# A fourth pair of split-weight buffers in place of the attention's features by token, and moved pick-ups, in a one-core hybrid decoder layer

## The chip, the core and the metric

One core of one Trainium2 chip. The metric is the device time of one launch in microseconds (us). The program uses TensorE (PE, with its weight loads shown as PEld), VectorE (DVE), ScalarE (ACT), GpSimd (POOL) and the DMA queues that SyncE (SP) and POOL feed.

## The reference

```python
def reference(x, ...):
    h = rms_norm(x, pre_norm_w)
    proj = h @ w_in                       # one projection, split in 8
    # A: gated DeltaNet: conv + SiLU on q, k, v; chunked delta rule
    #    (triangular solve per 64-chunk), gated RMSNorm
    oa = gated_delta_rule(l2(qa), l2(ka), va, beta, g)
    u_a = (rms(oa) * gdn_norm_w * silu(za)) @ w_branch_a
    # B: causal attention (one block of 256)
    ob = moba_attention(qb, kb, vb)
    u_b = (ob * silu(moba_z)) @ w_branch_b
    merged = sigmoid(gate_a) * u_a + sigmoid(gate_b) * u_b
    return x + rms_norm(merged @ w_out, post_norm_w)
```

256 tokens, model width 2048, 8 heads of 128 in each mixer, all float32.

## The kernel before

**Products.** Every large product is made of rounded halves: a number is its rounding hi plus the rest lo, and a product is hi·hi + hi·lo + lo·hi. The activations are kept in that form (hT, oaT, obT, mT). Weights are loaded in pieces of 1 MB (`raw_*`, three buffers, SP queue), and `split` (L215) makes of each half of a piece a pair: `hi_*` is a copy by ACT (L218), `lo_*` a difference by DVE (L219), both 128x1024. The pool `wspl` has three such pairs. TensorE then runs 12 matmuls of 512 columns on a pair (16 of 512 and 256 in `proj_t`), or 6 where only a quarter of the product is made. `mm` (L144) and `tr` (L147) pin TensorE's order; the copies and differences of `split` aren't pinned, and a list scheduler places them.

**Order of the work.** `ORDER` (L42) lists the blocks of the input projection. Beside them run queues (class `Queue`): `tick`, called after each half split, takes half a unit off each queue's wait and runs its next step when the wait is over. The DeltaNet's scores, its triangular inverse and its solve stand in `gq`, the attention's pairs of heads in `aq` and `bq`, the pick-ups of finished products in `dq`. The constants at the top are waits in units of two ticks.

**Triangular inverse** (`inverse`, L616). The triangles come back by DMA into `lc` on 32 partitions (`l_d`, L636). After `LC_WAIT` (L641), `copy` (L639, ACT, 1.05 us each) spreads them to the other partitions: three copies for the first 16 rows, further ones in steps 4, 7 and 10 of each 16. 63 steps of a product (L650, tw) and a difference (L657, tv) on DVE follow. The result goes to DRAM (`t_d`, L660) and back (`tt`, L666) by POOL's queue, and `solve` (L862) multiplies with it (`sv_*`, `so_*`).

**Attention** (`attend`, L1019). After `A_WAIT1` the scores `ms_*`, softmax on DVE and ACT (L1027 to L1033), after `A_WAIT2` the transposes `pp_*`, after `A_WAIT3` the values `po_*`; `turned_attention` (L1053) transposes the gated output (`pt_*`) into obT. Its features by token, `y_mq` and `y_mk`, lie in eight buffers of 1 KB (tag "f256"), which `halves` (L452) takes from the pool `wk`; L1072 multiplies the keys with rrow.

**Merged products** (`seven`, L776). Two by two blocks of a product are made from seven block products instead of eight. `branch_pair` (L825) runs it for columns 0 and 1 and again for 2 and 3 of the DeltaNet branch, with a gate projection (`ga3`, `gb2`) as fill between the seven; the output projection uses it once more. The weight differences `tq_*` are formed on DVE (L740), one of them inside `seven` by `fourth` (L792). `done` (L835) multiplies a finished product with its gate.

Of the kernel before, what the change touches and what calls it, by code (L numbers as in the profile page):

```python
# [8 lines left out]
F32 = mybir.dt.float32  # L9
F32R = mybir.dt.float32r  # L10
# [5 lines left out]
P = 128  # L16
# [8 lines left out]
D_WAIT = 7  # L25
SC_WAIT = 4
L_WAIT = 5
LC_WAIT = 2
INV = (0.6, 2)
SLOW = 8  # L30
T_WAIT = (5, 7, 7)
V_WAIT = 8
SV_WAIT = 1
OS_WAIT = 3
A_WAIT1 = 1
A_WAIT2 = 3
A_WAIT3 = 2
A_WAIT4 = 4
# [36 lines left out]
def hybrid_layer(  # L75
# [16 lines left out]
    B, S, D = x.shape  # L92
# [22 lines left out]
    wspl = ctx.enter_context(tc.tile_pool(name="wspl", bufs=3))  # L115
    wk = ctx.enter_context(tc.tile_pool(name="wk", bufs=2))
    dram = ctx.enter_context(tc.tile_pool(name="dram", bufs=1, space=bass.MemoryType.DRAM))
    acc = ctx.enter_context(tc.tile_pool(name="acc", bufs=4, space=bass.MemoryType.PSUM))
    aux = ctx.enter_context(tc.tile_pool(name="aux", bufs=4, space=bass.MemoryType.PSUM))

    def acc_tile(name):
        return acc.tile([P, 512], F32, tag="acc", name=name)
# [5 lines left out]
    aq, bq = [Queue(), Queue()], [Queue(), Queue()]  # L128
# [14 lines left out]
    def mm(*args, **kwargs):  # L143
        return pin(nc.tensor.matmul(*args, **kwargs))  # L144
# [67 lines left out]

    def split(raw, shape, name):  # L215
        hi = wspl.tile(shape, F32R, tag="hi", name=f"hi_{name}")
        lo = wspl.tile(shape, F32R, tag="lo", name=f"lo_{name}")
        nc.scalar.copy(hi, raw)  # L218
        nc.vector.tensor_tensor(lo, raw, hi.bitcast(F32), op=ALU.subtract)  # L219
        return hi, lo  # L220
# [94 lines left out]
    rrow = cst.tile([P, S], F32, name="rrow")  # L315
    prr = aux_tile("prr")
    for t in range(NT):
        dg = wk.tile([P, P], F32, tag="f256", bufs=8, name=f"dg_{t}")
        nc.vector.tensor_scalar_mul(dg, ident, rstd[:, t : t + 1])
        mm(prr[:, t * P : (t + 1) * P], ones, dg, start=True, stop=True)  # L320
    nc.vector.tensor_copy(rrow, prr[:, :S])
# [128 lines left out]


    def halves(pt, name):  # L452
        y = wk.tile([P, S], F32, tag="f256", bufs=8, name=f"y_{name}")
        nc.scalar.copy(y, pt[:, S:])
        nc.vector.tensor_tensor(y, pt[:, :S], y, op=ALU.add)
        return y
# [159 lines left out]
    def inverse():  # L616
        lc = big.tile([P, 64, 64], F32, tag="u1", name="lc")
        tv = big.tile([P, 16, 64], F32, tag="tv", name="tv")
        tw = big.tile([P, 16, 64], F32, tag="tw", name="tw")

        nc.gpsimd.memset(tv, 1.0)
        for g in range(4):
            nc.gpsimd.affine_select(
                out=tv[32 * g : 32 * g + 32],
                in_=tv[32 * g : 32 * g + 32],
                compare_op=ALU.is_equal,
                fill=0.0,
                base=g,
                pattern=[[4, 16], [-1, 64]],
                channel_multiplier=0,  # L630
            )

        rows = [slice(16 * r, 16 * r + 16) for r in range(4)]
        yield 0.5
        for js in rows:
            nc.gpsimd.dma_start(lc[0:32, js], l_d.rearrange("b h j i -> (b h) j i")[:, js])  # L636

        def copy(r, g):
            pin(nc.scalar.copy(lc[32 * g : 32 * g + 32, rows[r]], lc[0:32, rows[r]]))  # L639

        yield LC_WAIT  # L641
        for g in range(1, 4):
            copy(0, g)
        yield 0.5
        for j in range(63):
            if j < 48 and j % 16 in (4, 7, 10):
                copy(j // 16 + 1, (j % 16 - 1) // 3)
            n, r = j // 4 + 1, 63 - j
            pin(
                nc.vector.tensor_tensor(  # L650
                    tw[:, :n, :r],
                    lc[:, j : j + 1, j + 1 :].to_broadcast([P, n, r]),
                    tv[:, :n, j : j + 1].to_broadcast([P, n, r]),
                    op=ALU.mult,
                )
            )
            pin(nc.vector.tensor_tensor(tv[:, :n, j + 1 :], tv[:, :n, j + 1 :], tw[:, :n, :r], op=ALU.subtract))  # L657
            yield INV[after[0] > 0]
        for g in range(4):
            nc.gpsimd.dma_start(  # L660
                t_d.rearrange("b h (c g) i -> g (b h) c i", g=4)[g], tv[32 * g : 32 * g + 32]
            )
        inv.append(big.tile([P, NT, H, 64], F32, tag="tt", name="tt"))
        for p_ in range(2):
            for t in range(NT):
                nc.gpsimd.dma_start(  # L666
                    inv[0][p_ * 64 : p_ * 64 + 64, t, :, :], t_d[2 * t + p_].rearrange("h c i -> c h i")
                )
        yield L_WAIT
# [30 lines left out]
    def ga(c, t):  # L700
        return ga_[:, c, t, :]
# [48 lines left out]
    def product(a, raw, banks, first, name):  # L750

        for u in range(2):
            hi, lo = split(raw[:, 2 * u : 2 * u + 2, :], [P, 2, 512], f"{name}_{u}")
            for kk in range(2):
                k = 2 * u + kk
                for (ah, al), pt, new in zip(a, banks, first):
                    mm(pt, ah[:, k], hi[:, kk, :], start=(new and k == 0), stop=False, skip_group_check=True)
                    mm(pt, ah[:, k], lo[:, kk, :], start=False, stop=False, skip_group_check=True)
                    mm(pt, al[:, k], hi[:, kk, :], start=False, stop=(k == 3), skip_group_check=True)
                tick()  # L760
# [15 lines left out]
    def seven(quarter, s_, tq, w, c, banks, name, fill=lambda i: None, done=lambda b: None):  # L776
        c11, c12, c21, c22 = banks
        s5 = tq[0][:, 0]
        product([quarter(0, 0)], load(w, 0, c, name), [c21], [True], f"{name}p1")
        fill(0)  # L780
        product([s_[0]], tq[0], [c12], [True], f"{name}p5")
        nc.scalar.copy(c11, c21)
        product([s_[1]], tq[1], [c21], [False], f"{name}p6")

        dq.add(steps(lambda: nc.scalar.copy(s5, c12), lambda: nc.vector.tensor_tensor(c12, c21, s5, op=ALU.add)))
        fill(1)
        dq.drain()
        raw21 = load(w, 1, c, name)
        product([quarter(0, 1)], raw21, [c11], [False], f"{name}p2")
        product([s_[2]], tq[2], [c21], [False], f"{name}p7")  # L790

        def fourth(u):  # L792
            us = slice(2 * u, 2 * u + 2)
            pin(nc.vector.tensor_tensor(tq[1][:, us], raw21[:, us], tq[1][:, us], op=ALU.subtract))

        dq.add(
            steps(
                lambda: fourth(0),
                lambda: fourth(1),
                lambda: nc.vector.tensor_tensor(c22, c21, s5, op=ALU.add),  # L800
                lambda: done(c11),
            )
        )
        fill(2)
        product([s_[3]], load(w, 1, c + 1, name), [c12], [False], f"{name}p3")
        dq.drain()
        dq.add(steps(lambda: done(c12), lambda: done(c22)))
        fill(3)
        product([quarter(1, 1)], tq[1], [c21], [False], f"{name}p4")
        dq.add(later(lambda: done(c21)))  # L810
# [4 lines left out]

    def steps(*fs):
        for f in fs:
            f()
            yield 0.5

    def later(f):
        yield 1
        f()

    def branch_pair(i):  # L825
        c = 2 * i
        while not oas or c not in formed:
            sq.tick()
            gq.tick()
        c11, c12, c21, c22 = (acc_tile(f"a_ua{c}_{n}") for n in ("11", "12", "21", "22"))  # L830
        place = {id(c11): (c, 0), id(c12): (c + 1, 0), id(c21): (c, 1), id(c22): (c + 1, 1)}

        def done(b):
            cc, t = place[id(b)]
            nc.vector.tensor_tensor(ga(cc, t), ga(cc, t), b, op=ALU.mult)  # L835


        quarter = quarters(hT)
        n, g, col = (("ga", 3, CGA), ("gb", 2, CGB))[i]
        pts = [aux_tile(f"a_{n}{g}_{t}") for t in range(NT)]  # L840

        def gate(h):
            raw = load(w_in[:, col : col + D], h, g, n)
            product([quarter(0, h), quarter(1, h)], raw, pts, [h == 0] * 2, f"{n}{g}_{h}")
            if h == 3:
                for t in range(NT):
                    nc.scalar.activation(gate_place(n, g, t), pts[t], AF.Sigmoid, scale=rstd[:, t : t + 1])

        seven(quarters(oaT[0]), oas, tqs[-1], wa, c, (c11, c12, c21, c22), f"ua{c}", fill=gate, done=done)
# [169 lines left out]
    def attend(h, qT, kT):  # L1019
        yield A_WAIT1  # L1020
        ps = aux_tile(f"ms_{h}")
# [234 lines left out]
    for t in range(NT):  # L1256
        for k in range(KT):
            hi, lo = parts[k // 2][0][:, k % 2], parts[k // 2][1][:, k % 2]
# [35 lines left out]
```

## Time and profile before

| | before |
|---|---|
| median of 3 runs | 783.29 us (781.9 to 783.38) |
| profiled execution, its own time | 783.66 us |
| its span, first to last instruction | 781.7 us |
| mean granted TensorE clock | 0.996 |
| busy: PE, PEld, DVE, ACT, POOL | 765.8, 650.3, 564.2, 434.5, 33.5 us |
| DMA | 151.85 MB, mean 194 GB/s |

Times in rows are microseconds from the start of the span, unless a column is marked ns. A row of the timeline has start, duration, engine, line, operation, output<-inputs, shapes and count; in brackets stands the idle time of the engine before it and what ended it. A row of the waits has the engine and line, what it waited for, and then the sum, the number and the longest. A group row has count, busy time, mean ns of one, and the idle time before them with its main cause. The ends of matmuls are modelled: a 512-column matmul is shown with 0.39 us, though the next one starts 0.23 us after it, so stops are taken from start to start.

### The profile page before, as it was taken

To read this page: it belongs to the slowest core of one execution; us is meant where nothing else is said; L and a number is where in the kernel's file an instruction comes from. 1 tells how busy PE (TensorE), PEld (TensorE's weight loads), DVE (VectorE), ACT (ScalarE), POOL (GpSimd) and SP (SyncE) were. 2 spreads that over 40 slices of the span, in tenths; PEclk is the share of its full clock that TensorE was granted. 3 is DMA by queue.
4 is the path that set the end of the run, shared out by engine and by line. 5 is a ranking of instruction groups with operands and counts; after the bars stand their busy time and mean duration, and the time that the engine had idled before them with its cause. 6 is when DMAs were issued, how large, how long until landed. Compare 5 with 4: busy or idle time off the path is not lost.

```text
span 781.7 us, 10350 instructions
## 1 busy us (share of the span) xinstructions
PE 765.8 (98%) x3923; PEld 650.3 (83%) x3923; DVE 564.2 (72%) x914; ACT 434.5 (56%) x652; POOL 33.5 (4%) x61
## 2 busy tenths in 40 slices
PE   8999999999999999999999999999999999999995
PEld 7898988898788888888898888878887788887884
DVE  5787669885977898764547965675758677878753
ACT  5676665657656564553366474654455544556641
POOL 3000001112000000020001000000000000000000
PEclk9999999999999999999999999999999999999999
DMA  8576675467566556684348356657564965475822
GB/s 304 168 229 218 187 213 169 135 182 201 171 207 191 186 183 197 203 217 122 104 122 309 119 182 237 213 193 240 177 200 136 350 213 176 147 264 185 307 106 107
DMA packets 93655, 151.85 MB, mean 194 GB/s; under 512 B 3237, under 2 KB 46886, under 8 KB 93094
## 3 DMA queue, kind: packets, MB, share of 16 engines
q1 hardware_dynamic: 88902, 134.42, 53.8%
q0 software_dynamic: 4128, 15.74, 6.1%
q10 hardware_dynamic: 576, 1.05, 0.4%
q8 instruction: 30, 0.49, 0.3%
q14 instruction: 19, 0.16, 0.1%
HBM read 148.04 MB, written 3.15 MB: 193 GB/s over the span
## 4 chain that ended last, share of the span: by engine, by line
PE 89%; DVE 4%; ACT 4%; DMA 2%; issue 1%; SPq 0%; DVEq 0%; ACTq 0%
PE a_ga L144 11%; PE a_gb L144 11%; PE a_y L144 10%; PE a_k L144 6%; PE a_mk L144 6%; PE a_ub L144 6%; PE a_zm L144 6%; PE a_mq L144 5%; PE a_mv L144 5%; PE a_zg L144 5%; PE a_q L144 4%; PE a_v L144 4%; PE a_ua L144 3%; PE sv L144 2%; PE s L144 1%
## 5 line engine op out<-in xcount | busy, mean ns | idle before, releaser
L144 PE MATMUL a_ga<-hi_ga,hT 128*128 128x512 f32 x256 | 82.0, 393 | 0.0
L144 PE MATMUL a_gb<-hi_gb,hT 128*128 128x512 f32 x256 | 79.9, 389 | 0.0
L219 DVE TENSOR_TENSOR lo_gb<-raw_gb,hi_gb 128x1024 fp32r<-128x1024 f32 x32 | 38.8, 1223 | 26.6 <-ACT hi_gb L218 26.5
L144 PEld LDWEIGHTS a_gb<-hi_gb,hT 128*128 128x128 f32 x256 | 48.1, 188 | 9.9
L144 PEld LDWEIGHTS a_ga<-hi_ga,hT 128*128 128x128 f32 x256 | 48.1, 188 | 9.9
L219 DVE TENSOR_TENSOR lo_ga<-raw_ga,hi_ga 128x1024 fp32r<-128x1024 f32 x32 | 38.9, 1222 | 18.4 <-ACT hi_ga L218 18.2
L218 ACT CAST hi_gb<-raw_gb 128x1024 fp32r<-128x1024 f32 x32 | 33.3, 1052 | 33.3 <-PE a_gb L144 24.4
L144 PE MATMUL a_gb<-lo_gb,hT 128*128 128x512 f32 x128 | 50.5, 395 | 1.2 <-DVE lo_gb L219 1.1
L144 PE MATMUL a_ga<-lo_ga,hT 128*128 128x512 f32 x128 | 50.2, 392 | 1.0 <-DVE lo_ga L219 1.0
L218 ACT CAST hi_ga<-raw_ga 128x1024 fp32r<-128x1024 f32 x32 | 33.5, 1053 | 29.5 <-PE a_ga L144 15.4
L144 PE MATMUL a_zg<-hi_zg,hT 128*128 128x348 f32 (+1 forms) x192 | 47.0, 322 | 0.0
L144 PE MATMUL a_mk<-hT,hi_mk 128*128 128x512 f32 x128 | 46.5, 404 | 0.0
L144 PE MATMUL a_mq<-hT,hi_mq 128*128 128x512 f32 x128 | 46.4, 404 | 0.0
L144 PE MATMUL a_y<-hi_y,mT 128*128 128x512 f32 x144 | 45.9, 391 | 0.0
L144 PE MATMUL a_q<-hT,hi_q 128*128 128x512 f32 x128 | 45.8, 398 | 0.0
L144 PE MATMUL a_v<-hT,hi_v 128*128 128x512 f32 x128 | 45.2, 397 | 0.5 <-ACT hi_v L218 0.5
L144 PE MATMUL a_k<-hT,hi_k 128*128 128x512 f32 x128 | 41.2, 405 | 0.2 <-DVE hT L249 0.2
L144 PE MATMUL a_ub<-hi_ub,obT 128*128 128x512 f32 x128 | 41.1, 393 | 0.0
L144 PE MATMUL a_zm<-hi_zm,hT 128*128 128x512 f32 x128 | 40.6, 392 | 0.0
L144 PE MATMUL a_mv<-hi_mv,hT 128*128 128x512 f32 x128 | 40.1, 391 | 0.0
L144 PE MATMUL a_v<-hT,lo_v 128*128 128x256 f32 x128 | 36.0, 281 | 1.1 <-DVE lo_v L219 1.1
L144 PE MATMUL a_mq<-hT,lo_mq 128*128 128x256 f32 x128 | 35.9, 281 | 0.0
(377 smaller groups left out, 1973.2 us busy)
## 6 DMA issues: line engine op xcount, KB each, us to landing
raw_ga<-in_w_in_dram SPq DMA_DIRECT2D x16, 1024.0 KB, 5.2
raw_gb<-in_w_in_dram SPq DMA_DIRECT2D x16, 1024.0 KB, 6.2
raw_y<-in_w_out_dram SPq DMA_DIRECT2D x15, 1024.0 KB, 5.5
raw_q<-in_w_in_dram SPq DMA_DIRECT2D x8, 1024.0 KB, 5.8
raw_mv<-in_w_in_dram SPq DMA_DIRECT2D x8, 1024.0 KB, 5.2
raw_v<-in_w_in_dram SPq DMA_DIRECT2D x8, 1024.0 KB, 5.7
raw_zm<-in_w_in_dram SPq DMA_DIRECT2D x8, 1024.0 KB, 5.2
raw_mq<-in_w_in_dram SPq DMA_DIRECT2D x8, 1024.0 KB, 5.7
```

Source lines behind the costliest of these rows:

```text
L144: return pin(nc.tensor.matmul(*args, **kwargs))
L218: nc.scalar.copy(hi, raw)
L219: nc.vector.tensor_tensor(lo, raw, hi.bitcast(F32), op=ALU.subtract)
```

## The change

1. The 1 KB buffers (`f256`) move from `wk` to a pool `wf` of their own. At the first `branch_pair` the queues `aq` and `bq` are drained, `wf` is closed, and a pool `wx` of the same 8 KB is opened with one hi and one lo buffer. From then on every fourth `split` takes its pair from there.
2. `steps`, which runs the pick-ups one by one, waits half a unit before each of them instead of after it.
3. `LC_WAIT` goes from 2 to 3.5, and half a unit lies between the first copies instead of only behind them.
4. `A_WAIT1` goes from 1 to 1.5.
5. `fourth` inside `seven` is renamed `difference`.

The numbers of instructions are the same but for two more table loads on ACT and some semaphore waits.

```diff
-LC_WAIT = 2
+LC_WAIT = 3.5
...
-A_WAIT1 = 1
+A_WAIT1 = 1.5
...
+    early = ExitStack()
+    wf = early.enter_context(tc.tile_pool(name="wf", bufs=8))
...
+    splits, fourth = [0], []
+
     def split(raw, shape, name):
-        hi = wspl.tile(shape, F32R, tag="hi", name=f"hi_{name}")
-        lo = wspl.tile(shape, F32R, tag="lo", name=f"lo_{name}")
+        splits[0] += 1
+        pool = fourth[0] if fourth and splits[0] % 4 == 0 else wspl
+        hi = pool.tile(shape, F32R, tag="hi", name=f"hi_{name}")
+        lo = pool.tile(shape, F32R, tag="lo", name=f"lo_{name}")
...
-        dg = wk.tile([P, P], F32, tag="f256", bufs=8, name=f"dg_{t}")
+        dg = wf.tile([P, P], F32, tag="f256", name=f"dg_{t}")
...
-        y = wk.tile([P, S], F32, tag="f256", bufs=8, name=f"y_{name}")
+        y = wf.tile([P, S], F32, tag="f256", name=f"y_{name}")
...
         for g in range(1, 4):
             copy(0, g)
-        yield 0.5
+            yield 0.5
...
     def steps(*fs):
         for f in fs:
+            yield 0.5
             f()
-            yield 0.5
...
+        if not fourth:
+            for q in aq + bq:
+                q.drain()
+            early.close()
+            fourth.append(ctx.enter_context(tc.tile_pool(name="wx", bufs=1)))
```

More of the change, by code (lines that the diff above doesn't have):

```diff
@@ L790, in seven, with difference @@
         product([s_[2]], tq[2], [c21], [False], f"{name}p7")
-        def fourth(u):
+        def difference(u):
             us = slice(2 * u, 2 * u + 2)
@@ L797, in seven @@
             steps(
-                lambda: fourth(0),
-                lambda: fourth(1),
+                lambda: difference(0),
+                lambda: difference(1),
                 lambda: nc.vector.tensor_tensor(c22, c21, s5, op=ALU.add),
```

## The prediction

> **What bounds the kernel now.** I read the page first, then the waits of TensorE's weight loads, then TensorE's timeline at each place where those waits are long, and last the timelines of the engines named there.
>
> ```profile
> PE 765.8 (98%) x3923; PEld 650.3 (83%) x3923; DVE 564.2 (72%) x914; ACT 434.5 (56%) x652; POOL 33.5 (4%) x61
> ...
> PE 89%; DVE 4%; ACT 4%; DMA 2%; issue 1%; SPq 0%; DVEq 0%; ACTq 0%
> ...
> L219 DVE TENSOR_TENSOR lo_gb<-raw_gb,hi_gb 128x1024 fp32r<-128x1024 f32 x32 | 38.8, 1223 | 26.6 <-ACT hi_gb L218 26.5
> ...
> L218 ACT CAST hi_gb<-raw_gb 128x1024 fp32r<-128x1024 f32 x32 | 33.3, 1052 | 33.3 <-PE a_gb L144 24.4
> ```
>
> TensorE sets the end: 89% of the chain is its own. Matmuls are pipelined, so its 98% hides short stops, and the work of this change can only shorten those stops; no matmul is added or taken away. Each split of a weight piece costs ACT 1.05 us (the hi copy) and DVE 1.22 us (the lo difference) and feeds TensorE 12 matmuls or, in half the products of `seven`, 6. The last row says that ACT's hi copies idle 24.4 us until TensorE has released a buffer.
>
> [...]
>
> ```profile
> PEld a_gb L144 <- DVE lo_gb L219: 3.6, 6, 1.4
> PEld a_ga L144 <- DVE lo_ga L219: 2.1, 3, 1.4
> ...
> PEld a_v L144 <- DVE lo_v L219: 1.7, 2, 1.1
> PEld a_y L144 <- DVE lo_y L219: 1.6, 2, 1.2
> ```
>
> Nine microseconds in 13 waits, all for the lo half. A weight load waits a little longer than its matmul stops, so this bounds the loss from above. TensorE's timeline gives it from start to start; the five places are, in order of time:
>
> ```profile
> 195.39 0.28 PE L144 MATMUL a_v<-hT,lo_v 128*128 128x256 f32 x1
> 196.13 0.49 PE L144 MATMUL a_v<-hT,hi_v 128*128 128x512 f32 x1 [0.46 <-ACT hi_v L218]
> 197.39 0.39 PE L144 MATMUL a_v<-hT,lo_v 128*128 128x256 f32 x1 [0.77 <-DVE lo_v L219]
> ...
> 200.05 0.39 PE L144 MATMUL a_v<-hT,hi_v 128*128 128x512 f32 x1
> 200.77 0.39 PE L144 MATMUL a_v<-hT,lo_v 128*128 128x256 f32 x1 [0.33 <-DVE lo_v L219]
> ...
> 414.05 0.82 PE L144 MATMUL ms<-y_mk,y_mq 128*128 128x128 f32 x4
> 415.43 0.92 PE L144 MATMUL ms<-y_mk,y_mq 128*128 128x128 f32 x4 [0.56 <-DVE y_mk L1072]
> 416.19 0.72 PE L147 MATMUL pt<-ident,zm 128*128 128x128 f32 x4
> ...
> 513.40 0.39 PE L144 MATMUL a_ga<-hi_ga,hT 128*128 128x512 f32 x1
> 513.62 0.49 PE L144 MATMUL a_ga<-lo_ga,hT 128*128 128x512 f32 x1
> 513.96 0.63 PE L144 MATMUL a_ga<-hi_ga,hT 128*128 128x512 f32 x2
> ...
> 516.04 0.61 PE L144 MATMUL a_ga<-hi_ga,hT 128*128 128x512 f32 x2
> 517.63 0.50 PE L144 MATMUL a_ga<-lo_ga,hT 128*128 128x512 f32 x1 [0.97 <-DVE lo_ga L219]
> ...
> 602.75 0.61 PE L144 MATMUL a_gb<-hi_gb,hT 128*128 128x512 f32 x2
> 604.35 0.50 PE L144 MATMUL a_gb<-lo_gb,hT 128*128 128x512 f32 x1 [0.98 <-DVE lo_gb L219]
> ...
> 720.79 0.61 PE L144 MATMUL a_y<-hi_y,mT 128*128 128x512 f32 x2
> 722.15 0.50 PE L144 MATMUL a_y<-lo_y,mT 128*128 128x512 f32 x1 [0.75 <-DVE lo_y L219]
> ```
>
> 513.40 to 513.62 is an undisturbed step of 0.22 to 0.23 us, and a group "x2" is two such steps. So 517.63 - 516.04 - 0.45 = 1.14 us are lost, likewise 1.15 at 602.75 and 0.91 at 720.79; after each stop one slow step follows (513.62 to 513.96: 0.11 too much). With the shorter stops around them, added up in the same way, the three merged-gate stretches lose **C** 1.9 us (513 to 532), **D** 2.4 (578 to 619) and **E** 1.5 (683 to 722). The v block loses **A** 0.6 + 1.0 + 0.5 and two slow steps, 2.4. **B**: the ms matmuls of the third attention pair stop for 1.38 - 0.76 = 0.6 to 0.7 us, and by the same subtraction those of the fourth for about 0.25. In all 9.2 us.
>
> **Part 1, the fourth pair of buffers and the pick-ups (C, D, E).** What DVE did ahead of the stop at 517.63:
>
> ```profile
> 511.75 0.68 DVE L835 TENSOR_TENSOR ga<-ga,a_ua 128x512 f32<-128x512 f32 x1
> 512.35 1.22 DVE L219 TENSOR_TENSOR lo_ga<-raw_ga,hi_ga 128x1024 fp32r<-128x1024 f32 x1
> 513.48 2.36 DVE L794 TENSOR_TENSOR tq_z<-raw_ua,tq_z 128x1024 f32<-128x1024 f32 x2
> 515.75 0.69 DVE L800 TENSOR_TENSOR a_ua<-a_ua,tq_g 128x512 f32<-128x512 f32 x1
> 516.36 1.22 DVE L219 TENSOR_TENSOR lo_ga<-raw_ga,hi_ga 128x1024 fp32r<-128x1024 f32 x1
> ```
>
> DVE had no idle time here: a pick-up (0.68), then both `fourth` differences (2.36) and the sum c22 (0.61 beyond their overlap) stood ahead of the lo that TensorE needed. The change moves three things. With a fourth pair, hi can be copied one split earlier (1.36 or 2.72 us of TensorE). With `yield` ahead of each step, the 0.68 us multiply comes behind the lo of 512.35, and the 0.61 us sum behind the lo of 516.36; the two differences stay together ahead of it. So the late lo is ready 1.3 us earlier by the order alone, against 1.14 lost, and in the first split hi is no longer waiting, which feeds DVE sooner. In D the third raw buffer is in play as well:
>
> ```profile
> 602.62 5.17 DMA raw_gb<-in_w_in_dram
> ```
>
> This load waits for the buffer that the second difference reads, whose end comes about 2 us earlier, so it lands near 605.8 instead of 607.79, hi and lo follow by 608.2, and TensorE would want that lo at 608.3: just met. E has the order of C. I count 5.3 of the 5.8 us gained and leave 0.5 for that thin margin. The bounds are 5.8 and, if neither the buffer nor the order helps, 0. What is late next: nothing that TensorE reads here; DVE still has 1.22 us of every 1.36 us taken in a 6-matmul split, so the moved pieces (0.68, 0.61) must fit the 12-matmul splits, which have 1.5 us to spare each.
>
> To open the new pool all attention transposes are drained ahead of the first `branch_pair`. That issues the last two `pt` groups, 0.72 us of TensorE, 6 matmuls earlier, still 18 behind the last po; they are the same work, and their zm inputs are formed about 2 us before. Nothing is counted.
>
> **Part 2, the first copies (A).**
>
> ```profile
> 190.38 3.16 ACT L639 COPY lc<-lc 32x1024 f32<-32x1024 f32 x3 [2.21 <-DMA lc<-l_d]
> 193.56 0.37 ACT L454 COPY y_v<-a_v 128x256 f32<-128x256 f32 x1
> 193.96 1.05 ACT L639 COPY lc<-lc 32x1024 f32<-32x1024 f32 x1
> 195.03 1.05 ACT L218 CAST hi_v<-raw_v 128x1024 fp32r<-128x1024 f32 x1
> ```
>
> The diff says later and apart. In the order that the scheduler gives ACT, the three first copies stay together in the same place, still waiting for the same DMA, with hi_v and everything else on ACT queued behind them. Only the fourth copy (1.05 us) goes away, and DVE's first inverse steps move behind the lo. So hi_v ends 1.05 us earlier, at 195.03, its lo at about 196.3; TensorE, which can start hi at 195.5, stops once for 0.63 + 0.11. I count 1.6 of 2.4, bounds 0.5 (one stop stays whole) and 2.4.
>
> The copies' later start moves the inverse back by five half splits, and with it the solve, whose first matmuls are 40 product matmuls later. That is the place where this change can be late:
>
> ```profile
> 332.20 2.59 POOL L660 DMA_DIRECT2D t_d<-tv  x4 [145.03 <-DVE tv L657]
> 341.38 2.73 POOL L666 DMA_DIRECT2D tt<-t_d  x4 [6.59 <-ACT y_mk L454]
> ...
> 347.36 0.22 DVE L1033 RECIPROCAL sm<-sm 128x2 f32<-128x2 f32 x2
> ...
> 359.06 1.96 PE L144 MATMUL sv<-gdn,tt 64*64 64x128 f32 x16
> ```
>
> From the first store to the landed tt it takes 341.38 - 332.20 + 5.2 (the landing time above) = 14.4 us. The last tv step now stands behind the first pair's reciprocals, that is after 347.58 + one half split of 1.39 + its own 0.4 and a store's issue, about 350; tt lands near 364.4. The first sv matmul moves to 359.06 + 6.9 + the po group of 1.6, about 367.5. Three microseconds of cover are left of the 12.5 before. Counted at nothing; bounds 0 and 3.
>
> **Part 3, the attention one half split later (B).** ms, pp and po of all pairs come one half split (1.39 us) later. The third pair's stop of 0.7 goes, because y_mk is formed 3 us ahead there. In the fourth pair DVE gets two obT differences and three tq differences (1.22 each) ahead of the last y_mk product: I expect a stop of about 0.8 instead of 0.25, so -0.5; bounds +0.2 and -1.2 (one more 1.22 us difference ahead). Two more table loads arise, since the Sqrt of fo and the softmax's Exp now alternate:
>
> ```profile
> L1031 ACT ACT_TABLE_LOAD x2 | 2.6, 1283 | 0.0
> ```
>
> Two are 2.6 us of ACT. Around them ACT has the hi copy of the next split ready about 3.5 us ahead of TensorE by the order, so I count nothing; bounds 0 and 2.6.
>
> [...]
>
> **Sum.** 5.3 (C, D, E) + 1.6 (A) + 0.7 - 0.5 (B) = 7.1 us. The profiled execution took 783.66 us (span 781.7, the rest before and after it unchanged), which gives 776.6; the median of the runs, 783.29, is 0.4 lower, which gives **776.2**.
>
> **The rivals.**
> 1. *The fourth pair buys little.* DVE is the late engine, not the buffers: 1.22 us per lo in 1.36 us, and raw loads of 5.2 us through three raw buffers. Then C, D and E keep the two differences' 2.36 us ahead of a lo, and only 0.5 to 1 us comes of them; with A and B 2.3 to 2.8 in all, about 780.8. For it: DVE had no idle time in the rows of part 1. Against: 1.3 us of DVE work leaves the path by order alone.
> 2. *The inverse comes late: slower.* The last tv steps slip further behind softmax and lo work on DVE, and the first sv matmul, in TensorE's fixed order, holds every product queued behind it until tt has landed. Each microsecond past 367.5 costs one. It eats the gain at 374.6 and makes the kernel slower by over 1.6 us at 376.2, about 12 us later than I read it; then 785 to 788. For it: 9 of 12 us of cover are spent. Against: the order puts only the last step there, and the round trip is measured.
> 3. *The denser attention stage costs 2 to 4 us*: two table loads, the crowded fourth pair and transposes that share four PSUM banks. About 779.5 with the rest as forecast.
> 4. *The change doesn't do what it says.* For the first copies that is so by the order, and it is in the sum: "apart" is not reached.
>
> **How the numbers follow.** What a measurement of this kernel can tell from no change is 0.2%, 1.6 us: 781.7 to 784.9 is the same. The forecast has 0.60 (774 to 778.5), all of it faster. Rival 1 has 0.18: 0.12 faster, 0.04 same, 0.02 slower. Rival 2 has 0.12: 0.03 faster, 0.01 same, 0.08 slower. Rival 3 has 0.10: 0.05 faster, 0.02 same, 0.03 slower. Together faster 0.80, same 0.07, slower 0.13. The range starts where every stop of the 9.2 us goes and the fourth pair's too (783.3 - 9.4 = 773.9), and ends at 782.0, behind rival 1 and the milder half of rival 3; what lies above is the slower cases and part of the same ones, under 0.2.
>
> **What would show it.** Right: in the waits of TensorE's weight loads the rows for lo_ga, lo_gb and lo_y fall from 7.3 together to under 1.5; a_v keeps one stop of about 0.6; the ms row stays near 1 but belongs to the fourth pair; two more table loads of 1.28 us. Rival 1 would leave those three rows above 4. Rival 2 would show a new row, sv waiting for the DMA tt, of several microseconds. Rival 3 would show waits of a_mq, a_mk, pp or ms between 340 and 450. Wrong outright: a row of waits of TensorE that none of these names, above all for hi (ACT) where the fourth pair is first used, or at 484 to 492, where the drained transposes stand.

## The result, and the profile after

The changed kernel takes 778.01 us (median of 5 runs, 776.93 to 779.23) against 782.8 of the kernel before: the ratio is 0.9937, interval 0.9923 to 0.995. On a second occasion it was 777.63 against 783.23, 0.9934 (0.992 to 0.9947). So it is 4.8 to 5.6 us faster; 7.1 were forecast. Its profiled execution took 777.05 us, 6.6 less than that of before.

The page of the changed kernel, the busy line and the chain:

```profile
PE 763.5 (98%) x3923; PEld 650.2 (84%) x3923; DVE 565.2 (73%) x914; ACT 436.1 (56%) x654; POOL 33.5 (4%) x61
...
PE 95%; ACT 2%; DVE 2%; DMA 1%; SPq 0%; issue 0%; DVEq 0%
```

TensorE's share of the chain has gone from 89% to 95%. The waits of its weight loads that were long before (lines are 3 to 12 higher than in the kernel before):

```profile
PEld ms L147 <- DVE y_mk L1084: 1.1, 1, 1.1
...
PEld a_ga L147 <- DVE lo_ga L226: 0.5, 1, 0.5
```

The rows for lo_gb, lo_v, lo_y and hi_v are gone altogether; lo_ga has fallen from 2.1 to 0.5, and that one is a new place. From start to start, as in the prediction, TensorE's stops of before and after are:

| place | before | changed |
|---|---|---|
| v block (A) | 2.4 | 0 |
| third attention pair (B) | 0.7 | 0 |
| fourth attention pair (B) | 0.25 | 0.85 |
| start of the ua0 stretch, at 488.8 us | 0 | 0.35 |
| merged-gate stretches (C, D, E) | 5.8 | 0 |

That is 8.0 us of stops less. Two further things stand beside them in the profile's 6.6. One is chance, at the start. The first of x came at the same time in both: the second group of hTp began at 6.10 us before and at 6.11 in the changed kernel, the first a_k product at 8.21 and 8.23. But the granted clock from 7 to 11 us was 0.50 to 0.70 in the profile of before and 1.00 in the other. So the first 16 a_k matmuls took 4.06 us there and 2.87 here; from there to the next a_k product it is 0.79 and 1.14 us, which gives 0.35 back, since the hTp group between them waits in the changed kernel for x until 11.46. The first zg product in the chain, of before and of the changed kernel:

```profile
35.72 15.34 PE a_zg L144 x96
```

```profile
34.89 15.35 PE a_zg L147 x96
```

Nothing in the change touches this part; 0.8 us of the profile's gain is this. The other is a loss of 1.8 us that no row of waits shows. In the timeline of the changed kernel's TensorE, the starts of the lo matmuls in gb, each three matmuls apart:

```profile
530.64 0.39 PE L147 MATMUL a_gb<-lo_gb,hT 128*128 128x512 f32 x1
...
531.34 0.39 PE L147 MATMUL a_gb<-lo_gb,hT 128*128 128x512 f32 x1
...
532.04 0.39 PE L147 MATMUL a_gb<-lo_gb,hT 128*128 128x512 f32 x1
...
534.81 0.39 PE L147 MATMUL a_gb<-lo_gb,hT 128*128 128x512 f32 x1
...
535.49 0.39 PE L147 MATMUL a_gb<-lo_gb,hT 128*128 128x512 f32 x1
...
536.17 0.39 PE L147 MATMUL a_gb<-lo_gb,hT 128*128 128x512 f32 x1
```

0.70 us for three matmuls in the first group, 0.68 in the second. The slow steps, 233 ns instead of 227, come here in runs of 12 matmuls, one run in every 48: exactly one split in four, that is, the splits in the new fourth pair. There are 29 of them, 18 with 12 matmuls and 11 with 6, so 282 matmuls; at 6.3 ns each that is 1.8 us (the expectation of the run 64 bytes lower, below, takes all 29 with 12 and comes to 2.3). 8.0 + 0.8 - 1.8 = 7.0. Of the 0.4 us that are left over, no run shows the reason; the products of `proj_t` are longer in this profile, 351.9 ns on average for a step of 512 and one of 256 columns together, against 350.6 (the 520 or so such pairs of steps under 400 ns), which comes to 0.7 us.

### The profile page after: what moved, and what is told of

It reads as the page before. It is cut to its first block, busy times and chain, and to the rows that moved or that the text cites. A ratio compares the mean times of both kernels' runs of the same rounds, so it can differ in the third digit from the quotient of the medians.

```text
span 775.4 us, 10348 instructions
## 1 busy us (share of the span) xinstructions
PE 763.5 (98%) x3923; PEld 650.2 (84%) x3923; DVE 565.2 (73%) x914; ACT 436.1 (56%) x654; POOL 33.5 (4%) x61
## 4 chain that ended last, share of the span: by engine, by line
PE 95%; ACT 2%; DVE 2%; DMA 1%; SPq 0%; issue 0%; DVEq 0%
PE a_gb L147 11%; PE a_y L147 11%; PE a_ga L147 11%; PE a_zg L147 6%; PE a_mq L147 6%; PE a_v L147 6%; PE a_mk L147 6%; PE a_ub L147 6%; PE a_zm L147 6%; PE a_mv L147 5%; PE a_k L147 5%; PE a_ua L147 5%; PE a_q L147 4%; PE sv L147 2%; PE s L147 1%; DMA x<-in_x_dram 1%
## 5 line engine op out<-in xcount | busy, mean ns | idle before, releaser
L225 ACT CAST hi_gb<-raw_gb 128x1024 fp32r<-128x1024 f32 x32 | 33.3, 1051 | 35.6 <-PE a_gb L147 26.5
L147 PE MATMUL a_q<-hT,lo_q 128*128 128x256 f32 x128 | 35.9, 281 | 0.0
```

## The experiments

The runs were made in three sets, each with the kernel before beside it; its medians there are 783.23, 783.18 and 783.22 us. So runs of different sets are set against each other here, and the changed kernel counts with 777.63, the median of its second measurement.

**The changed kernel again.**

> The changed kernel once more, unedited. Open is why its five runs lie between 776.9 and 779.2 us while its profiled execution, 777.05, shows hardly a stop. Theory: the lc transfer decides; it landed at 189.06 us in that profile, 0.9 us earlier against TensorE than before, and each microsecond that it lands later stops TensorE in the v block again. Then a profile with a time near 778 to 779 has a stop of 0.5 to 1.5 us at 193 to 196. Rival: no stop comes back, and the difference lies in slightly longer steps between matmuls everywhere, or at the start of the program (x transfer, up to 0.8 us).

777.63 us (777.52 to 778.01). The theory fell: lc landed at 189.92 here, no stop came back in the v block, and the stops are those of the first profile. The rival held in its last part, the start of the program, but not by the x transfer: the second group of hTp began at 6.09 us here and at 6.11 in the first profile, and its seven matmuls took 1.76 us instead of 0.98. The first zg product of this run, and that of the run with the old `steps` below (776.6 us in its profile):

```profile
35.46 15.34 PE a_zg L147 x96
```

```profile
34.61 15.34 PE a_zg L147 x96
```

This run is 0.58 us longer than the first profile (777.05), and 0.57 us of it are there at the first zg product. So most of the difference between these profiles is the start; for runs without a profile that isn't shown.

**Without the fourth pair.**

> The changed kernel with all splits in the three pairs again; the drain, the closed pool and the order of pick-ups stay. Theory (the prediction's working): putting the pick-ups behind the lo takes 1.3 us of DVE off the path where 1.14 were lost, so the order alone brings most; 0.5 to 1.5 us slower than the changed kernel, and the lo_ga, lo_gb, lo_y rows in the waits of TensorE's weight loads come to 1 to 2 us. Rival: hi copied earlier is what frees DVE; then 3.5 to 5.4 us slower and those rows back at 5 to 7.

```diff
-        pool = fourth[0] if fourth and splits[0] % 4 == 0 else wspl
+        pool = wspl
```

781.15 us (780.01 to 782.58), ratio to before 0.9979 (0.997 to 0.9989): 3.5 slower than the changed kernel. Its waits of TensorE's weight loads:

```profile
PEld a_gb L147 <- DVE lo_gb L226: 3.5, 6, 1.1
PEld a_ga L147 <- DVE lo_ga L226: 2.6, 4, 1.0
...
PEld a_y L147 <- DVE lo_y L226: 1.0, 2, 0.6
```

7.1 together, against 7.3 before; 0.5 of the 7.1 is the new stop at ua0. From start to start, the three merged-gate stretches lose 5.2 us here, against 5.8 before. The rival held: the later pick-ups by themselves take away 0.6 us. The timeline of its DVE in the stretch that the prediction quoted:

```profile
510.42 0.68 DVE L847 TENSOR_TENSOR ga<-ga,a_ua 128x512 f32<-128x512 f32 x1
511.02 1.22 DVE L226 TENSOR_TENSOR lo_ga<-raw_ga,hi_ga 128x1024 fp32r<-128x1024 f32 x1
512.15 2.35 DVE L801 TENSOR_TENSOR tq_z<-raw_ua,tq_z 128x1024 f32<-128x1024 f32 x2
514.42 1.22 DVE L226 TENSOR_TENSOR lo_ga<-raw_ga,hi_ga 128x1024 fp32r<-128x1024 f32 x1
515.56 0.69 DVE L807 TENSOR_TENSOR a_ua<-a_ua,tq_g 128x512 f32<-128x512 f32 x1
```

Only the sum c22 went behind the second lo; the multiply still stands ahead of the first, and hi still waits for a buffer, so two stops of 1.14 and 0.17 have become two of 0.54 and 0.79. With the fourth pair, the same stretch of the changed kernel:

```profile
508.31 1.22 DVE L226 TENSOR_TENSOR lo_ga<-raw_ga,hi_ga 128x1024 fp32r<-128x1024 f32 x1
509.45 2.35 DVE L801 TENSOR_TENSOR tq_z<-raw_ua,tq_z 128x1024 f32<-128x1024 f32 x2
511.72 1.22 DVE L226 TENSOR_TENSOR lo_ga<-raw_ga,hi_ga 128x1024 fp32r<-128x1024 f32 x1
512.85 0.69 DVE L807 TENSOR_TENSOR a_ua<-a_ua,tq_g 128x512 f32<-128x512 f32 x1
513.46 0.68 DVE L847 TENSOR_TENSOR ga<-ga,a_ua 128x512 f32<-128x512 f32 x1
```

The same DVE work, but earlier against TensorE. The first matmul that reads this lo starts at 511.39 here and at 512.30 without the pair, so the lo starts 3.1 us ahead of it instead of 1.3. Its hi is copied 3.9 us ahead of its first matmul instead of 2.5, one split of 6 matmuls earlier. The scheduler then puts the multiply last.

**With the old `steps`.**

> The changed kernel with steps() waiting after each pick-up as before; the fourth pair stays. Theory (order brings most): 2 to 4 us slower, with stops of 0.5 to 1 us in the merged-gate stretches. Rival (the fourth pair brings most): within 1 us of the changed kernel, and no stop over 0.3 us there.

```diff
-            yield 0.5
             f()
+            yield 0.5
```

777.59 us (776.6 to 779.04), as the changed kernel, and no stop over 0.2 us in the merged-gate stretches C, D and E. Here too the multiply stands behind the second lo, though `steps` is the old one. The rival held: the pick-ups' place is worth nothing once the fourth pair is there.

**With the old first copies.**

> The changed kernel with LC_WAIT 2 and the first copies' spacing as before. Theory: the fourth copy comes back ahead of hi_v, so the v block's stops come back: 1.6 us slower as predicted, up to 2.2 if the two profiles' difference is all due to the edit. Rival: the lc transfer came earlier by chance in the profile of the changed kernel and the edit is worth under 0.5 us.

```diff
-LC_WAIT = 3.5
+LC_WAIT = 2
...
             copy(0, g)
-            yield 0.5
+        yield 0.5
```

778.75 us (778.57 to 779.18), 1.1 slower than the changed kernel. The v block's stops are back, 0.78 + 0.46 and two slow steps, 1.5 us in its profile. Between the first mk product and ua0 about 0.5 of that is given back, where the fourth attention pair's stop is gone (see below). Part of the 2.4 us of before was chance. The first three copies in the timelines of ACT before and in the changed kernel, with the wait for their transfer in brackets:

```profile
190.38 3.16 ACT L639 COPY lc<-lc 32x1024 f32<-32x1024 f32 x3 [2.21 <-DMA lc<-l_d]
```

```profile
189.06 3.17 ACT L646 COPY lc<-lc 32x1024 f32<-32x1024 f32 x3 [1.34 <-DMA lc<-l_d]
```

The wait was 1.3 to 1.7 us in the five profiles told of so far since the change, 2.2 in the one of before. The stops follow it wherever the copies are the old ones: with waits of 1.3, 1.6 and 1.8 us, in the three runs below that only move buffers of the kernel before, the v block loses 1.4, 1.7 and 1.9 us.

**The fourth pair 64 bytes lower.**

> The changed kernel with its fourth pair 64 bytes lower in SBUF (a small tile ahead of it shares another's place): 221088 and 225184 bytes per partition instead of 221152 and 225248, so 32 past a multiple of 128 as the three other pairs are, instead of 96. In the changed kernel's profile the 12 matmuls on every fourth split follow each other at 233 ns, those on the others at 227; 29 splits of 12 by 6.6 ns are 2.3 us. Theory 1 (the place in memory): all splits at 227, and 2.0 to 2.3 us faster than the changed kernel, about 775.5. Rival 1 (a fourth pair as such: ACT and DVE write it while TensorE reads): every fourth split stays at 233 and the time stays at 777.6. Rival 2 (the high address): as rival 1.

```diff
-        rs = wk.tile([P, 1], F32, tag="rstd", name=f"rs_{t}")
+        rs = wk.tile([P, 2], F32, tag="sm", name=f"rs_{t}")[:, 0:1]
```

777.1 us (776.88 to 777.82): 0.5 faster than the changed kernel's repeat. Every fourth split is still slow, 232 ns on average, but in another pattern (near 229 and 237 in turn); the long gb piece in the chain took 43.87 us, against 43.92 in the changed kernel. The theory as stated, the place modulo 128, fell; that the pattern changed with 64 bytes kept the place in question.

**The kernel before with its pairs 64 bytes higher.**

> The kernel before with 64 bytes set aside ahead of its three pairs (and one small tile at the end sharing another's place), so that all pairs lie 96 past a multiple of 128 instead of 32. Nothing else is moved against them but the small tiles behind. Theory 1 (the place in memory): all 512-column matmuls that stream a split, some 1800, go from 227 to 233 ns, 11 to 12 us more less what the three pairs' stops give back, so 790 to 795. Rivals (a fourth pair as such, or its high address): 783.2 unchanged.

```diff
+    pad = ctx.enter_context(tc.tile_pool(name="pad", bufs=1)).tile([P, 16], F32, name="pad")
+    nc.gpsimd.memset(pad, 0.0)
     wspl = ctx.enter_context(tc.tile_pool(name="wspl", bufs=3))
...
-        rs = wk.tile([P, 1], F32, tag="rstd", name=f"rs_{t}")
+        rs = wk.tile([P, 2], F32, tag="sm", name=f"rs_{t}")[:, 0:1]
```

787.08 us (785.96 to 787.82), ratio 1.0053 (1.004 to 1.0066): 3.9 us slower with three pairs and no fourth, so a fourth pair as such isn't the cause. The size was missed: the steps average 229 ns, not 233 (90 of them in ga took 20.61 us in the chain, 20.43 before).

**With the old wait before the scores, and with it for the last pair alone.**

> The changed kernel with A_WAIT1 at 1 as before. Theory (the prediction's working): the third pair's stop of 0.7 us comes back and the fourth's falls from 0.84 to about 0.25, so 0.1 us slower, within 0.5 of the changed kernel. Rival: the half split matters elsewhere too (ua0's first split, the solve), then over 1 us either way.

> The changed kernel with the fourth pair 64 bytes lower and with the wait before the scores of the fourth pair of heads at 1, of the others at 1.5. Theory: 2.0 to 2.3 us from the place and 0.6 from the fourth attention pair's stop, so about 774.9, below both kernels. Rival: the last pair's y_mk is as late with the shorter wait and the stop stays, or the place gives nothing: 775.5 or 777.6.

The edits are `A_WAIT1 = 1`, and `yield 1 if h >= 6 else A_WAIT1` together with the 64 bytes. 778.56 us (778.09 to 778.83) and 777.42 (776.49 to 778.37). Both theories missed. In both profiles the fourth attention pair's stop is longer, 1.3 us, and the third pair has none. With the old copies and the new wait neither pair has a stop. So the third pair's stop goes by the later copies or by the later scores, either of which is enough; and the later copies are what makes the fourth pair's stop, which the longer wait then shortens. With the copies the solve's start moves, from 358.5 us to 365; that it is the solve which does this is likely, but no run moves it alone.

**The fourth pair in phase.** In the kernel before, hT, the other stationary operands and all three pairs lie 288 bytes past a multiple of 512. The fourth pair lies 480 past, in the run 64 lower 416, and in the run with all pairs moved 352. These places are read from the programs' allocations, not from a trace. Streamed is here the operand of 128x512 in the row of a matmul, stationary the one of 128x128 in the row of its weight load (PEld); in these products the program passes the split as the streamed one.

> The changed kernel with its fourth pair at 220960 and 225056 bytes per partition (one small junk tile has one buffer instead of two, and 64 bytes are set aside), so that it lies 288 past a multiple of 512, as the three other pairs and hT do. So far 96 or 192 bytes off gave 233 ns steps and 64 off gave 229 on average. Theory 2 (what counts is the place modulo 512 against the other operand): every split at 227, 2.0 to 2.3 us faster than the changed kernel, about 775.4. Rival (the high address, or a fourth pair as such): every fourth split stays at 233, 777.5.

```diff
-        jk = wk.tile([P, P], BF16, tag="jk", name=f"jk_{h}")
+        jk = wk.tile([P, P], BF16, tag="jk", bufs=1, name=f"jk_{h}")
...
+    pad = wk.tile([P, 16], F32, tag="pad", bufs=1, name="pad")
+    nc.gpsimd.memset(pad, 0.0)
     early = ExitStack()
```

775.68 us (774.8 to 777.08), ratio 0.991 (0.9897 to 0.9924): 2.0 faster than the changed kernel, and the splits are at 227 ns, all but 36 matmuls. Those read sums of parts of oaT or mT as the stationary operand, and the smaller junk tile has moved these sums 192 bytes down. They take 233 ns (2.80 us for 12 in the chain, 2.72 for others), 24 of them with splits in the three old pairs. So neither the high address nor a fourth pair as such is needed for slow steps. The long gb piece in the chain, of the changed kernel and of this one:

```profile
527.85 43.92 PE a_gb L147 x192
```

```profile
527.08 43.52 PE a_gb L149 x192
```

**In phase, and the last pair's scores later.**

> As the run before it, and the wait before the scores of the fourth pair of heads is 2, of the others 1.5. Theory: the fourth attention pair's stop of 0.84 us goes, since y_mk is formed within one half split, so 0.7 to 0.8 less, about 774.7. Rival: the later scores push softmax into the lo differences behind them and a new stop of 0.5 to 1 us comes there; then no gain.

The edit besides is `yield 2 if h >= 6 else A_WAIT1`. 775.07 us (773.87 to 775.6), ratio 0.9897 (0.9882 to 0.9912), the fastest here. The ms row is gone from the waits of TensorE's matmuls, and what is left in them belongs to the start (among its weight loads, the short wait for lo_ga at ua0 is still there):

```profile
PE hTp L152 <- DMA x<-in_x_dram: 1.4, 2, 0.8
PE warm L149 <- DVE epst L183: 1.1, 1, 1.1
```

The gain over the run before it, 0.6 us, has the expected size, but the two intervals overlap; the profile shows that the stop is gone, the times alone don't.

**All 64 bytes higher, and the pairs 128 higher.**

> The kernel before with 64 bytes set aside ahead of everything, so that the pairs, hT, oaT, obT and mT all move by 64 together. In the run with the pairs alone moved by 64 the matmul steps were 229 ns on average and the time 787.1. Theory 2a (the place of the streamed operand against the stationary one): back to 227, 783.2. Theory 2b (the place alone, modulo 512): 229 as with the pairs alone, about 787.

> The kernel before with the three pairs 128 bytes higher, everything else in place. Theory 2: as the fourth pair 128 off in the run where it lay 64 lower, 232 to 233 ns steps in some 1800 matmuls, 10 to 12 us more, about 794. Rival (only being off counts, not how far): 229 ns as with 64, about 787. Rival (multiples of 128 are all alike): 227, 783.2.

The edits are the `pad` ahead of the first pool (with the small tile sharing another's place), and a `pad` of 32 columns ahead of `wspl` (with one jk buffer). 783.21 us, ratio 1.0 (0.9991 to 1.0009), and 790.93, ratio 1.0104 (1.009 to 1.0117). The long gb piece in the chain of the kernel before, of the run with all moved, with the pairs 64 higher, and with the pairs 128 higher:

```profile
531.88 43.59 PE a_gb L144 x191
```

```profile
530.14 43.59 PE a_gb L146 x191
```

```profile
534.71 44.01 PE a_gb L146 x191
```

```profile
534.60 45.02 PE a_gb L146 x192
```

Theory 2a held: moved together, the steps are 227 ns again (43.59 us, as the 43.59 of before); 64 apart they are 229, 128 apart 233. The forecast for 128 was 10 to 12 us and 7.7 came: some 1730 steps are 5.4 ns longer, 9.4 us, but slower matmuls also shorten the stops, of which the profile has 2.0 us less than that of before.

## Why the prediction was right or wrong

The forecast, 776.2 us with faster the likeliest, held in sign and within its range; the first median is 1.8 above it. By its steps:

- **What bounds the kernel**: right. The time followed TensorE's stops, and the waits of its weight loads named the places. ACT's idle time promised nothing by itself: in the changed kernel its copies of hi_gb still wait for a_gb, 26.5 us against 24.4, and TensorE's stops in gb are gone.
- **C, D, E, 5.3 us**: the size was right (5.8 less the new stop of 0.35), the split of the credit wrong. The prediction said that the order alone takes 1.3 us off the path where 1.14 were lost. Undone, the order costs nothing; the fourth pair undone costs 3.5 us: 5.2 us of stops come back, and the 1.8 us of slow steps go. The step that failed took the scheduler's order of the changed kernel for the work of `steps`. With the pair and the old `steps` the multiply stands last too; with the new `steps` and no pair it stands first. So it is the earlier hi that lets the scheduler choose this order.
- **A, 1.6 us**: 1.5 by the profile with the copies undone. Here the working was right. That no stop was left in the changed kernel's profiles fits the transfer, whose copies began 0.6 to 0.9 us earlier against the v block than in the profile of before; no profile of the changed kernel has it as late as there, so the one stop of 0.6 was neither seen nor ruled out.
- **B, 0.7 - 0.5**: both stops came out as said (0.7 gone, 0.25 to 0.85), but for another cause: not the half split of A_WAIT1 but the later copies, with the later inverse and solve, move DVE's work into the fourth pair. The wait, worth 0.2 us by the forecast, gains about 0.5 to 0.9 us beside those copies. That the fourth pair's stop came out at the size said is luck.
- **The cover of tt**: right. 3 us were said to be left; the tt loads were issued from 353.96 on and sv began at 365.09:

```profile
353.96 2.74 POOL L673 DMA_DIRECT2D tt<-t_d  x4 [3.70 <-PE a_mk L147]
```

  They took 4.4 to 6.6 us from issue to landing, where the prediction put in the 5.2 of a weight piece. The last of the four landed at 362.6, so 2.5 us were left, and no row of sv waiting for a transfer appears. The inverse is not late.
- **The table loads at nothing**: right. They are there (L1043 x3 and L937 x2, two more than before, 1283 ns each), and no wait of TensorE names them. ACT loses hardly more than the 1283 ns to each: the idle time ahead of all three loads of L1043 is 0.1 us together, behind 16 of the trace's 18 loads ACT's next instruction starts within 0.02 us, and behind the other two it waits 0.84 and 1.12 us for DVE's mx.
- **The drained transposes at nothing**: a term missed. A stop of 0.35 us came at 488.8, in the place that the prediction named for it. The chain there runs over ACT, the sigmoid of ga, obT and hi_ga, then lo_ga:

```profile
485.08 1.17 ACT ga L728 x2
...
486.35 0.64 ACT obT L1073 x2
486.99 0.96 ACT hi_ga L225
```

  The stop is there in every run of the changed kernel, whichever of the pair, `steps`, the copies or the wait is taken back, and in none of the kernel before. So the drain is the likely cause; draining later wasn't tried.
- **What the sum lacked**: 1.8 us for reading the fourth pair. The prediction took 227 ns for every matmul and looked for the cost of the new pool in waits. The allocation, 221152 bytes against 186144, could be read from the program, but the kernel before streams no 512-column split in another phase, so its trace had no row to price it by.

Stops of 7.1 were forecast to go, 8.0 went by the two profiles, and 1.8 came back by slower steps: 6.2. Of that, 0.5 to 1 us is the transfer's chance in the v block, which leaves 5.2 to 5.7, against the 4.8 and 5.6 measured. The forecast's miss, 1.4 to 1.8 us, is about the term that the sum lacked.

## What to carry to other kernels

Look at the place of a buffer that is added to a ring, which was worth 2.0 us here: compare the step from matmul to matmul buffer by buffer, since the slower one, 233 ns instead of 227, showed in no row of waits and in no granted clock (1.00 from 528 to 572 us in the changed kernel). Where a list scheduler sets the order, undo each edit by itself before giving one of them the credit; here one of four brought most, one nothing, and two changed each other's worth. And compare kernels that differ by 1 us over runs, not by one profile: the start alone moved by 0.8 us.

## What the runs showed of the hardware

The step between 512-column matmuls that stream a split changed with the place of the split in SBUF against the stationary operand. With the distance between the two taken modulo 512 bytes, the profiles show 227 ns at 0, 229 at 64 (the pairs 64 higher), 232 to 233 at 128 (the fourth pair 64 lower, the pairs 128 higher) and 233 at 192 (the changed kernel). The same 90 matmuls of ga took 20.43 us in the chain before, 20.61 with the pairs 64 higher, 20.92 with 128, and 20.43 again with the pairs and the stationary operands both moved by 64. The 36 matmuls that lie 256 bytes apart in the run with the pairs 128 higher took 229 on average; 12 of them stand in its chain with 2.76 us. That the distances repeat after 512 bytes is the author's reading of these places; no run tests it by itself.

In the pieces compared of other products the times didn't rise. Where the split is stationary and hT is streamed (`proj_t`), the 64 matmuls of an mq piece took 11.31 us in the chain before and with the pairs 64 higher, 11.23 with 128. The first two zg pieces, each of 96 matmuls of 344 or 348 columns, took 15.34 and 15.36 us before, 15.30 and 15.21 with the pairs 64 higher, 15.27 and 15.22 with 128.

The mean granted clock is 0.996 to 0.998 in all profiles here. What makes the steps longer was not shown.
